# Memory tokens loaded transposed, with the norm's row factor applied behind the products, in a two-layer hybrid decoder on one core

## The chip, the cores and the metric

The kernel runs on one core of one Trainium2 chip. The metric is the device time of one execution in microseconds (us), as the median of three runs. The profile is of one execution. The engines are PE (matrix products; PEld is its weight load), DVE (vector), ACT (scalar, activations), POOL (GpSimd) and SP, which here issues most of the transfers.

## The reference, cut to what matters

All inputs are f32. `x` is 512 x 1024, `mem` is 256 x 1024.

```
mem_n = rmsnorm(mem, mem_norm_g)          # mem * rsqrt(mean(mem^2, row) + 1e-6) * g
for i in (0, 1):                          # layer 0: FoX attention; layer 1: retention
    h = rmsnorm(x, norm_g[i])
    q, k, v, (f_logit), q_mem, z = split(h @ w_in[i])
    main = fox_attention(...) or retention(...)          # 12 heads of 128
    kv = mem_n @ w_mem_kv[i]; km, vm = split(kv)         # 4 heads of 128 each
    memo = softmax(q_mem @ km.T / sqrt(128)) @ vm        # per head, 256 memory tokens
    x = x + (concat(main, memo) * silu(z)) @ w_out[i]
return rmsnorm(x, final_norm_g)
```

The change touches `mem_n`, `km` and `vm` alone. The row factor `rsqrt(mean + eps)` is one number for each memory token, and the gain `g` one for each of the 1024 channels.

## The kernel before

Each f32 product is made of three products of rounded parts: an operand is split into a high part H (a cast to the type float32r) and a low part L (the operand minus H), and `split3` lists (H, H), (H, L), (L, H). `split_to` does such a split with an ACT cast and a DVE subtraction.

Weights come as pieces of 128 x 1024 (512 KB) in the order of their use. `load_piece` has SP issue the load of the next piece into one of three raw buffers. `prep_piece` casts a raw piece to wH on ACT (L127), subtracts on DVE to wL (L128; four buffers of each) and then calls `load_piece`, whose transfer waits for the raw buffer. `retire` is called when PE is through with a piece, and prepares a further one.

The program is a list of cycles. A cycle is a list of filler chunks (dense products for PE) and of jobs that are put between the chunks at given positions; a job at position p is emitted behind the chunk in which p lies. PE's order is the order of emission, by hand (`MANUAL`). SP's is by hand during the first two cycles, and that of DVE, ACT and POOL in the opening block of `emit` (L795 to L801). All else on these three engines is placed by the scheduler, by priority and readiness.

The opening: `start_mem` issues the loads of the norm gain (as two rows of one partition), of the two halves of `mem` (128 tokens each, tokens on partitions), of the identity (`csb`) and of three pieces, and has POOL broadcast the gain to all partitions (L683). 13 products on zeros warm PE up (L794). `mem_norm(b)` calls `normed`: ACT squares the half and sums each row (L167), POOL makes the row factor with a TENSOR_SCALAR (L168) and a power (L169), and DVE multiplies by factor and gain (L170). `mem_T(b)` transposes the half on PE in eight blocks (L177) and splits it from PSUM into the tiles `mT` (L148, L149), which have channels on partitions.

The first cycle has eight chunks for layer 1: four of the values (`f_vm`, L387, 12 products of 512 columns each, in an order in which token half 0 comes first) and four of the keys (`f_km`, L59 by way of `mm_group`, 24 products of 256 columns each). The second half's transposes (`mem1`) are a job at position 1.5, and the loads of the first norm's gain and of `x` are jobs from position 2.5 on (`xload`). Layer 1's keys and values are written to DRAM for later. The second cycle has the same products for layer 0 and, between them, the norms and transposes of `x`. Then layer 0 begins.

Of the kernel before, what the change touches and what calls it, by code (L numbers as in the profile page):

```python
# [8 lines left out]
F32 = mybir.dt.float32  # L9
# [23 lines left out]


@with_exitstack
def tile_hybrid(ctx, tc, x_in, mem_in, norm_g, mem_g, fin_g, b_f, wv0, wp, index, consts, cosT, sinT, dec, out):
    nc = tc.nc
    P = 128
    KD = D // P
# [34 lines left out]
    def tile_(tag, shape, dt=F32):  # L74
        return work.tile(shape, dt, name=tag, bufs=BUFS[tag])

    csb = cst.tile([P, P], F32, name="csb")
    ident = csb[:, 0:P]
    nhalf = cst.tile([P, 1], F32, name="nhalf")
    G.memset(nhalf, -0.5)  # L80
# [15 lines left out]
    def load_g(ap):  # L96
        return load(ap.partition_broadcast(P))

# [1 line left out]
    order = []  # L100
    raws, pieces = {}, {}
    nload, nprep = [0], [0]
# [16 lines left out]
    def prep_piece():  # L119
        i = nprep[0]  # L120
        if i < len(order):
            key = order[i]
            n = 1072 if is_v0(key) else 1024
            raw = raws.pop(key)
            H = wpool.tile([P, 1072], F32R, name="wH", bufs=BUFS["w"])
            L = wpool.tile([P, 1072], F32R, name="wL", bufs=BUFS["w"])
            A.copy(out=H[:, :n], in_=raw[:, :n])  # L127
            V.tensor_tensor(out=L[:, :n], in0=raw[:, :n], in1=H[:, :n].bitcast(F32), op=ALU.subtract)  # L128
            pieces[key] = (H, L)
            nprep[0] += 1  # L130
            load_piece()
# [10 lines left out]
        retire(*retired)  # L142
        retired.clear()

# [13 lines left out]

    def acc_tile():
        return ps_at("acc", [P, 512], F32, name="acc")  # L160

    def normed(src, g, dst):
        ss = small.tile([P, 1], F32, name="ss")
# [22 lines left out]
                                    hL[:, hf * 4:hf * 4 + 4, t * P:(t + 1) * P], slice(0, 4))])  # L186
        yield

# [1 line left out]
    def f_T(key, done):  # L190
        box = {}

# [159 lines left out]
    def f_km(l, h):  # L352
        key = (l, "km", h)

        def fn():
            H, L = pieces[key]
            mT = st["mT"]
            ps = acc_tile()
            terms = []
            for w, c in ((H, 0), (H, 1), (L, 0)):  # L360
                for k in range(KD):
                    terms.append((w[:, k * P:(k + 1) * P], mT[k][c]))
            mm_group(ps[:, :NMEM], terms)
            kt = tile_("km", [P, 2, NMEM], F32R)
            split_to(kt[:, 0, :], kt[:, 1, :], ps[:, :NMEM])
            st[l, "km", h] = kt
            if l == 1:
                nc.sync.dma_start(out=km_d[h], in_=kt.bitcast(F32))
            retire(key)
        return [([key], fn)]  # L370

    def f_vm(l, plan):
        box = {}
        seen = {}

        def part(steps, final):
            mT = st["mT"]
            for i, b in steps:
                H, L = pieces[l, "vm", i]
                if b not in box:  # L380
                    box[b] = acc_tile()
                n = 0
                for k2 in range(2):
                    k = 2 * i + k2
                    for a, w in split3(mT[k][0][:, b * P:(b + 1) * P], mT[k][1][:, b * P:(b + 1) * P],
                                       H[:, k2 * 512:(k2 + 1) * 512], L[:, k2 * 512:(k2 + 1) * 512]):
                        PE.matmul(box[b], lhsT=a, rhs=w, start=(i == 0 and n == 0), stop=(i == 3 and n == 5))  # L387
                        n += 1
                seen[i] = seen.get(i, 0) + 1
                if seen[i] == 2:  # L390
                    retire((l, "vm", i))
            if final:
                vm = [tile_("vv", [P, 2, 512], F32R) for _ in range(2)]
                for b in range(2):
                    split_to(vm[0][:, b, :], vm[1][:, b, :], box[b])
                st[l, "vm"] = vm
                if l == 1:
                    for c in range(2):
                        nc.sync.dma_start(out=vm_d[c], in_=vm[c].bitcast(F32))
        res, used = [], set()  # L400
        for steps in plan:
            keys = [(l, "vm", i) for i, _ in steps if i not in used]
            keys = list(dict.fromkeys(keys))
            used.update(i for i, _ in steps)
            res.append((keys, lambda steps=steps, f=steps is plan[-1]: part(steps, f)))
        return res
# [13 lines left out]
            G.dma_start(out=vm[c], in_=vm_d[c])  # L420
        st[1, "vm"] = vm

# [175 lines left out]
    def g_forget():  # L598
# [42 lines left out]
        ret2=(0, 1, 2, 3, 5, 6, 8, 12),  # L641
        forget=(0, 2, 3),
        norm=(0, 2),
        mem1=(0,),
        xload=(0, 1, 2, 3, 4),
    )
    def mem1_gen():
        mem_T(1)
        prep_piece()
        yield  # L650

    GEN = dict(mem=g_mem, fox=g_fox, ret=g_ret, ret2=g_ret, forget=g_forget, norm=norm_gen, mem1=mem1_gen, xload=lambda: xload_gen())

    cycles = []
    tail_jobs = []
# [6 lines left out]
    def cycle(fillers, jobs=(), start=None, mode=None, last=False):  # L662
        cycles.append((fillers, jobs, start, mode, last))
# [2 lines left out]
        return [(kind, (l, h), base + i * gap) for i, h in enumerate(heads)]  # L666

    def start_mem():
        g1 = tile_("dd", [1, D // 2]), tile_("dd", [1, D // 2])
        for i in range(2):  # L670
            nc.sync.dma_start(out=g1[i], in_=mem_g[i * 512:(i + 1) * 512].unsqueeze(0))
        src = []
        for b in range(2):
            src.append(load(mem_in[b * P:(b + 1) * P, :]))
            if b == 0:
                nc.sync.dma_start(out=csb, in_=consts[:, 0:P])
                load_piece()
        for _ in range(BUFS["raw"] - 1):
            load_piece()
        st["msrc"] = src  # L680
        st["mg"] = tile_("vv", [P, D])
        for i in range(2):
            G.partition_broadcast(st["mg"][:, i * 512:(i + 1) * 512], g1[i])  # L683
        mT = [[tile_("gg", [P, 2, NMEM], F32R) for _ in range(2)] for _ in range(4)]
        st["mTt"] = mT
        st["mT"] = [(m[0][:, k, :], m[1][:, k, :]) for m in mT for k in range(2)]

    def mem_norm(b):
        xn = tile_("vv", [P, D])
        normed(st["msrc"][b], st["mg"], xn)  # L690
        st["mxn", b] = xn

    def mem_T(b):
        mT = st["mTt"]
        cs = slice(b * P, (b + 1) * P)
        transposes(st["mxn", b], lambda hf: [(mT[hf * 2 + k][0][:, :, cs], mT[hf * 2 + k][1][:, :, cs],
                                              slice(2 * k, 2 * k + 2)) for k in range(2)])

    def xload_gen():
        st["g", 0] = load_g(norm_g[0])  # L700
        yield
        for t in range(NT):
            nc.sync.dma_start(out=xt[t], in_=x_in[t * P:(t + 1) * P, :])
            yield

    def build_layer(l):
        M = "fox" if l == 0 else "ret"
        fq = (lambda pr: f_q(0, "q", pr * 2, NEG_SCALE) + f_q(0, "k", pr * 2, None) +
# [9 lines left out]
        for pr in range(6):  # L718
# [67 lines left out]
    def emit():  # L786
# [6 lines left out]
        for i in range(WARM):  # L793
            PE.matmul(wps, lhsT=warm[:, :P], rhs=warm, start=(i == 0), stop=(i == WARM - 1))  # L794
        with tc.manual_schedule(engines={mybir.EngineType.DVE, mybir.EngineType.Pool, mybir.EngineType.Activation}):  # L795
            mem_norm(0)
            prep_piece()
            mem_T(0)
            prep_piece()
            mem_norm(1)  # L800
            prep_piece()  # L801
# [145 lines left out]
```

## Time and profile before

| what | us |
|---|---|
| median of three runs | 962.19 (961.83 to 962.3) |
| span of the profiled execution, first to last instruction | 959.9 |
| PE busy in it | 932.4 (97%) |
| DVE busy | 592.2 (62%) |
| ACT busy | 435.5 (45%) |
| POOL busy | 36.8 (4%) |

The profiled execution was timed by its span only; 2.3 us lie between that and the median of the runs. A row of the timeline gives the start, the busy time, the engine, the line, the operation with its output and inputs and a count, and in brackets the idle time before it with what ended it. A row of groups gives the busy time and the mean duration of one in ns. A row of windows gives for each engine the busy time and the number of instructions, then PE's granted clock, the share of the DMA engines and the rate in GB/s.

### The profile page before, as it was taken

Reading aid. Unit: us, or ns where it says so; the run is one execution under the profiler, and the core shown is the slowest. Engines: PE = TensorE matmul, PEld = TensorE weight load, DVE = VectorE, ACT = ScalarE, POOL = GpSimd, SP = SyncE. Lnnn points to the kernel's source line nnn. Section 1 sums busy time; section 2 is a strip of 40 time slices with the busy share of each in tenths; the row PEclk is TensorE's granted clock in tenths of the full one; section 3 lists DMA queues with packets and bytes.
Section 4 is the critical chain, followed back from the end, with each engine's and each line's share of the span. In section 5 each row is a group of like instructions: output and inputs, shape, how many; then the busy total and the mean of one; then the engine's idle time right before and its main releaser. Section 6 shows DMA issues by size and latency. Waiting matters only on the chain.

```text
span 959.9 us, 13070 instructions
## 1 busy us (share of the span) xinstructions
PE 932.4 (97%) x5017; PEld 799.4 (83%) x5017; DVE 592.2 (62%) x1035; ACT 435.5 (45%) x746; POOL 36.8 (4%) x94
## 2 busy tenths in 40 slices
PE   3999999999999999999999999999999999999995
PEld 2899888888889889898888898888889889888984
DVE  2676655555655536645547766567768476856776
ACT  2564444432433324433425344455447354744554
POOL 1020100000000000000000010000000000000001
PEclk7999999999999999999999999999999999999998
DMA  4684322222323223222232242323332343333202
GB/s 140 244 316 138 127 82 97 98 78 83 103 79 99 78 89 90 86 67 99 99 109 79 66 154 67 106 71 98 99 99 77 99 121 108 113 99 97 91 23 88
DMA packets 32058, 99.69 MB, mean 104 GB/s; under 512 B 4206, under 2 KB 4462, under 8 KB 31996
## 3 DMA queue, kind: packets, MB, share of 16 engines
q1 hardware_dynamic: 30556, 95.72, 30.7%
q0 software_dynamic: 864, 2.10, 0.8%
q10 hardware_dynamic: 576, 1.05, 0.3%
q8 instruction: 39, 0.64, 0.3%
q14 instruction: 23, 0.19, 0.1%
HBM read 91.48 MB, written 4.22 MB: 100 GB/s over the span
## 4 chain that ended last, share of the span: by engine, by line
PE 95%; issue 2%; ACT 1%; DVE 1%; POOL 1%; DMA 0%; POOLq 0%; DVEq 0%; ACTq 0%
PE acc L201 44%; PE acc L59 33%; PE s L59 6%; PE o L491 5%; PE acc L387 2%; PE pt L525 1%; PE o L59 1%; PE pt L177 1%; PE pt L460 1%; PE acc L334 1%; PE acc L328 1%; ACT dd L762 0%; DVE p L565 0%; ACT vv L773 0%; DVE x L291 0%
## 5 line engine op out<-in xcount | busy, mean ns | idle before, releaser
L128 DVE TENSOR_TENSOR wL<-raw,wH 128x1024 fp32r<-128x1024 f32 x148 | 181.0, 1224 | 137.3 <-ACT wH L127 79.2
L127 ACT CAST wH<-raw 128x1024 fp32r<-128x1024 f32 x148 | 154.8, 1049 | 111.4 <-PE acc L201 54.6
L201 PE MATMUL acc<-hL,wH 128*128 128x512 f32 x608 | 164.3, 396 | 0.0
L201 PE MATMUL acc<-hH,wH 128*128 128x512 f32 x608 | 154.8, 396 | 0.0
L201 PE MATMUL acc<-hH,wL 128*128 128x512 f32 x608 | 152.4, 393 | 0.0
L59 PE MATMUL acc<-wH,gg 128*128 128x512 f32 x448 | 147.6, 397 | 0.0
L201 PEld LDWEIGHTS acc<-hH,wL 128*128 128x128 f32 x608 | 114.3, 188 | 26.1
L201 PEld LDWEIGHTS acc<-hL,wH 128*128 128x128 f32 x608 | 111.3, 188 | 21.9
L201 PEld LDWEIGHTS acc<-hH,wH 128*128 128x128 f32 x608 | 111.0, 188 | 22.1
L59 PE MATMUL acc<-wH,hH 128*128 128x256 f32 (+1 forms) x384 | 108.7, 283 | 0.0
L59 PE MATMUL acc<-wL,hH 128*128 128x256 f32 (+1 forms) x384 | 107.9, 281 | 0.0
L59 PE MATMUL acc<-wH,hL 128*128 128x256 f32 (+1 forms) x384 | 107.7, 280 | 0.0
L59 PEld LDWEIGHTS acc<-wH,gg 128*128 128x128 f32 x448 | 84.2, 188 | 18.4
L59 PE MATMUL acc<-wL,gg 128*128 128x512 f32 x224 | 88.2, 394 | 0.0
L291 DVE TENSOR_TENSOR x<-acc,x 128x512 f32<-128x512 f32 x80 | 55.0, 689 | 43.5 <-PE acc L59 41.3
L59 PEld LDWEIGHTS acc<-wL,hH 128*128 128x128 f32 x384 | 72.3, 188 | 0.5
L59 PEld LDWEIGHTS acc<-wH,hH 128*128 128x128 f32 x384 | 72.3, 188 | 0.5
L59 PEld LDWEIGHTS acc<-wH,hL 128*128 128x128 f32 x384 | 72.3, 188 | 0.0
L515 ACT ACTIVATE p<-dd,nm 128x128 f32<-128x128 f32 (+3 forms) x48 | 27.0, 563 | 66.6 <-DVE nm L511 66.5
L148 ACT CAST pTH<-pt 128x128 fp32r<-128x128 f32 (+2 forms) x64 | 29.7, 465 | 57.5 <-PE pt L525 44.6
L59 PE MATMUL s<-qk 128*128 128x256 f32 (+3 forms) x240 | 54.4, 327 | 0.6 <-DVE p L565 0.6
L148 ACT CAST gg<-sz 128x512 fp32r<-128x512 f32 x32 | 19.9, 621 | 75.7 <-PE acc L59 32.3
(148 smaller groups left out, 1190.0 us busy)
## 6 DMA issues: line engine op xcount, KB each, us to landing
raw<-in_wp_dram SPq DMA_DIRECT2D x146, 512.0 KB, 3.5
cbc<-c_d SPq DMA_DIRECT2D x12, 256.0 KB, 3.2
cbc<-in_dec_dram SPq DMA_DIRECT2D x12, 256.0 KB, 3.8
dd<-dd SPq DMA_DIRECT2D x48, 64.0 KB, 2.0
x<-in_x_dram SPq DMA_DIRECT2D x4, 512.0 KB, 8.4
raw<-in_wv_dram SPq DMA_DIRECT2D x2, 536.0 KB, 3.9
vv<-in_mem_dram SPq DMA_DIRECT2D x2, 512.0 KB, 4.6
vv<-in_norm_g_dram SPq DMA_DIRECT2D x2, 512.0 KB
```

The lines of the kernel that those rows point to most:

```text
L59: PE.matmul(ps, lhsT=l, rhs=r, start=(i == 0), stop=(i == n - 1))
L127: A.copy(out=H[:, :n], in_=raw[:, :n])
L128: V.tensor_tensor(out=L[:, :n], in0=raw[:, :n], in1=H[:, :n].bitcast(F32), op=ALU.subtract)
L148: A.copy(out=dH, in_=src)
L177: PE.transpose(pt[:, k, :], xn[:, c:c + P], ident)
L201: PE.matmul(box["ps"], lhsT=a[:, k * P:(k + 1) * P], rhs=b[:, k, :], start=(n == 0), stop=(n == 23))
L291: V.tensor_tensor(out=dst, in0=ps, in1=dst, op=ALU.add)
L328: PE.matmul(ps, lhsT=a, rhs=b, start=(i == 0), stop=False)
L334: PE.matmul(ps, lhsT=a, rhs=b, start=False, stop=(i == 2))
L387: PE.matmul(box[b], lhsT=a, rhs=w, start=(i == 0 and n == 0), stop=(i == 3 and n == 5))
L491: PE.matmul(o[:, j * P:], lhsT=a, rhs=b, start=(j == 0 and i == 0), stop=(j == NT - 1 and i == 2))
L515: A.activation(p[:, :n], dd[:, :n], AF.Exp, bias=nm, scale=-1.0, accum_out=sm)
```

## The change

`mem` is given to the kernel a second time, transposed on the host into two tiles of 128 x 4 x 256 (channels on partitions), and the gain as 128 x 8 columns. The transposed tiles are split as they land, with the gain as a factor for each partition, straight into `mT`. Products with them lack the row factor. That is computed from the row layout of `mem`, which is still loaded, behind the pieces; `rstd_of` makes one factor for each token half, and the values are split from PSUM with it as a scale for each partition. For the keys, whose tokens lie on the free axis, `spread` lays both factors out as a row on all partitions with two f32 products, and DVE multiplies by it (into `kn`) before the split. This runs as a job (`memr`) at position 1.5, where `mem1` stood. The values' chunks go piece by piece, both token halves in each. The `xload` jobs begin at position 0.5. Comments were taken out as well.

```
 def start_mem():
-    g1 = tile_("dd", [1, D // 2]), tile_("dd", [1, D // 2])
-    for i in range(2):
-        nc.sync.dma_start(out=g1[i], in_=mem_g[i * 512:(i + 1) * 512].unsqueeze(0))
-    src = []
-    for b in range(2):
-        src.append(load(mem_in[b * P:(b + 1) * P, :]))
-        if b == 0:
-            nc.sync.dma_start(out=csb, in_=consts[:, 0:P])
-            load_piece()
+    nc.scalar.dma_start(out=gc, in_=g_cols)
+    src = [tile_("vv", [P, 4, NMEM]) for _ in range(2)]
+    rows = [tile_("vv", [P, D]) for _ in range(2)]
+    nc.sync.dma_start(out=src[0], in_=memT_in[0])
+    load_piece()
+    nc.sync.dma_start(out=src[1], in_=memT_in[1])
     for _ in range(BUFS["raw"] - 1):
         load_piece()
-    st["mg"] = tile_("vv", [P, D])
-    for i in range(2):
-        G.partition_broadcast(st["mg"][:, i * 512:(i + 1) * 512], g1[i])
+    nc.sync.dma_start(out=csb, in_=consts[:, 0:P])
+    for b in range(2):
+        nc.sync.dma_start(out=rows[b], in_=mem_in[b * P:(b + 1) * P, :])
...
-def mem_norm(b):
...
-def mem_T(b):
...
+def mem_split(k):
+    dH, dL = st["mT"][k]
+    split_to(dH, dL, st["msrc"][k // 4][:, k % 4, :], gc[:, k:k + 1])
+
+def memr_gen():
+    st["mr"] = [rstd_of(st["mrows"][b], st["mrows"][b], f"mr{b}") for b in range(2)]
+    spread(st["mr"], rbm)
+    yield
...
+def rstd_of(src, junk, name):
...
+    A.activation(junk, src, AF.Square, accum_out=ss)
+    G.tensor_scalar(out=r, in0=ss, scalar1=1.0 / D, scalar2=EPS, op0=ALU.mult, op1=ALU.add)
+    G.tensor_tensor(out=r2, in0=r, in1=nhalf, op=ALU.pow)
+    return r2
+
+def spread(rs, dst):
+    pb = ps_at("t", [P, 4, P], F32, name="pt")
+    for i, r in enumerate(rs):
+        PE.matmul(pb[:, i, :], lhsT=r.to_broadcast([P, P]), rhs=ident, start=True, stop=True)
+    n = len(rs)
+    A.copy(out=dst[:, :n * P], in_=pb[:, :n, :].rearrange("p n c -> p (n c)"))
...
 # f_km
-            split_to(kt[:, 0, :], kt[:, 1, :], ps[:, :NMEM])
+            kn = tile_("dd", [P, 512])
+            V.tensor_tensor(out=kn[:, :NMEM], in0=ps[:, :NMEM], in1=rbm, op=ALU.mult)
+            split_to(kt[:, 0, :], kt[:, 1, :], kn[:, :NMEM])
 # f_vm
-                    split_to(vm[0][:, b, :], vm[1][:, b, :], box[b])
+                    split_to(vm[0][:, b, :], vm[1][:, b, :], box[b], st["mr"][b])
...
-    cycle(f_vm(1, [[(0, 0), (1, 0)], [(2, 0)], [(0, 1), (1, 1)], [(2, 1), (3, 0), (3, 1)]]) +
-          sum([f_km(1, h) for h in range(4)], []), [("mem1", (), 1.5), ("xload", (), 2.5)], mode=8)
+    cycle(f_vm(1, [[(i, 0), (i, 1)] for i in range(4)]) +
+          sum([f_km(1, h) for h in range(4)], []), [("memr", (), 1.5), ("xload", (), 0.5)], mode=8)
...
 # emit, with DVE, POOL and ACT in hand order
-            mem_norm(0)
-            prep_piece()
-            mem_T(0)
-            prep_piece()
-            mem_norm(1)
-            prep_piece()
+            for i in range(4):
+                mem_split(2 * i)
+                mem_split(2 * i + 1)
+                prep_piece()
```

## Rows read from the trace of the kernel before

**Rows 1.** The page: PE's busy tenths in 40 slices, and the chain by engine.
```profile
PE   3999999999999999999999999999999999999995
...
PE 95%; issue 2%; ACT 1%; DVE 1%; POOL 1%; DMA 0%; POOLq 0%; DVEq 0%; ACTq 0%
```

**Rows 2.** Windows: the stretch behind the opening.
```profile
29.93:950.00 920.07, 918.63 (x4969) 789.51 (x4970) 578.32 (x1017) 422.84 (x724) 31.60 (x77) 1.00 0.32 102
```

**Rows 3.** Windows: two stretches of the opening.
```profile
6.40:18.60 12.20, 0.00 (x0) 0.00 (x0) 1.33 (x2) 1.04 (x1) 2.26 (x4) 0.58 0.35 138
18.60:29.93 11.33, 8.51 (x35) 6.32 (x35) 7.50 (x10) 5.64 (x10) 0.74 (x2) 0.85 0.40 123
```

**Rows 4.** Timeline of the opening, all engines.
```profile
4.82 1.06 ACT L167 ACTIVATE vv<-vv 128x1024 f32<-128x1024 f32 x1 [2.82 <-DMA vv<-in_mem_dram]
...
7.33 1.04 ACT L127 CAST wH<-raw 128x1024 fp32r<-128x1024 f32 x1 [1.36 <-DMA raw<-in_wp_dram]
7.83 1.48 POOL L683 PARTITION_BROADCAST vv<-dd  x2 [6.98 <-issue]
16.37 0.18 POOL L168 TENSOR_SCALAR rstd<-ss 128x1 f32<-128x1 f32 x1 [7.06 <-issue]
...
18.47 1.22 DVE L128 TENSOR_TENSOR wL<-raw,wH 128x1024 fp32r<-128x1024 f32 x1
...
18.61 1.97 PE L177 MATMUL pt<-csb,vv 128*128 128x128 f32 x8 [12.31 <-DVE vv L170]
```

**Rows 5.** Timeline of SP: its issues.
```profile
0.73 0.65 SPq L671 DMA_DIRECT2D dd<-in_mem_norm_g_dram  x2
1.42 0.35 SPq L93 DMA_DIRECT2D vv<-in_mem_dram  x1
...
4.83 0.56 SPq L810 DMA_DIRECT2D bfb<-in_fox_b_f_dram  x1
19.71 15.99 SPq L115 DMA_DIRECT2D raw<-in_wp_dram  x6
```

**Rows 6.** Timeline: layer 1's first key products, and a row factor of x.
```profile
36.99 2.07 PE L59 MATMUL acc<-gg,wH 128*128 128x256 f32 x16
...
50.39 0.19 ACT L167 ACTIVATION_READ_ACCUMULATOR vv<-x 128x1 f32 x1
...
50.94 0.55 POOL L169 TENSOR_TENSOR rstd<-rstd,nhalf 128x1 f32<-128x1 f32 x1
```

**Rows 7.** Groups by shape, 0 to 72 us.
```profile
L128 DVE TENSOR_TENSOR wL<-raw,wH 128x1024 fp32r<-128x1024 f32 x16 | 19.4, 1222 | 6.0 <-ACT wH L127 6.0
L127 ACT CAST wH<-raw 128x1024 fp32r<-128x1024 f32 x16 | 16.6, 1051 | 7.7 <-DMA raw<-in_wp_dram 5.9 <-PE acc L387 1.2 <-PE acc L59 0.7
...
L149 DVE TENSOR_TENSOR km<-acc,km 128x256 fp32r<-128x256 f32 x8 | 3.3, 417 | 0.0
...
L148 ACT CAST km<-acc 128x256 fp32r<-128x256 f32 x8 | 2.9, 366 | 0.7 <-PE acc L59 0.7
```

**Rows 8.** Groups by shape, whole span, ACT.
```profile
L773 ACT ACTIVATE vv<-vv,rstd 128x512 f32<-128x512 f32 x4 | 2.9, 719 | 2.7 <-POOL rstd L768 2.7
```

**Rows 9.** DMA view, 0 to 12 us, in 40 slices: rate, and what moved.
```profile
GB/s 0 0 0 0 0 7 7 0 96 177 314 410 410 336 333 369 341 328 273 150 205 150 177 355 437 410 396 382 396 423 410 437 410 430 397 289 173 3 0 0
DMA packets 1156, 2.83 MB, mean 236 GB/s; under 512 B 258, under 2 KB 514, under 8 KB 1156
```

**Rows 10.** Windows: the first 72 us and stretches of it.
```profile
0.00:72.00 72.00, 55.44 (x335) 48.75 (x336) 40.06 (x49) 35.64 (x55) 9.73 (x22) 0.91 0.67 233
30.00:72.00 42.00, 42.00 (x288) 38.80 (x289) 30.67 (x38) 26.46 (x41) 6.41 (x10) 1.00 0.84 299
30.00:36.80 6.80, 6.80 (x30) 5.44 (x31) 5.33 (x8) 4.79 (x7) 0.00 (x0) 1.00 0.54 179
48.40:61.40 13.00, 13.00 (x114) 13.00 (x113) 8.79 (x13) 10.21 (x19) 4.81 (x9) 1.00 0.97 373
61.40:72.00 10.60, 10.60 (x53) 8.80 (x52) 9.40 (x11) 5.97 (x8) 1.60 (x2) 1.00 0.79 242
```

More of the change, by code (lines that the diff above doesn't have):

```diff
@@ L35, in tile_hybrid @@
 @with_exitstack
-def tile_hybrid(ctx, tc, x_in, mem_in, norm_g, mem_g, fin_g, b_f, wv0, wp, index, consts, cosT, sinT, dec, out):
+def tile_hybrid(ctx, tc, x_in, mem_in, memT_in, g_cols, norm_g, fin_g, b_f, wv0, wp, index, consts, cosT, sinT, dec, out):
     nc = tc.nc
@@ L77, in tile_hybrid @@
     csb = cst.tile([P, P], F32, name="csb")
+    gc = cst.tile([P, KD], F32, name="gc")
+    rbm = cst.tile([P, NMEM], F32, name="rbm")
     ident = csb[:, 0:P]
@@ L160, in acc_tile @@
         return ps_at("acc", [P, 512], F32, name="acc")
+    def rstd_of(src, junk, name):
+        ss = small.tile([P, 1], F32, name="ss")
+        r = small.tile([P, 1], F32, name="rstd")
+        r2 = small.tile([P, 1], F32, name=name, bufs=1)
+        A.activation(junk, src, AF.Square, accum_out=ss)
[8 more added lines that the diff above has]
+        A.copy(out=dst[:, :n * P], in_=pb[:, :n, :].rearrange("p n c -> p (n c)"))
     def normed(src, g, dst):
@@ L643, in tile_hybrid @@
         norm=(0, 2),
-        mem1=(0,),
+        memr=(0,),
         xload=(0, 1, 2, 3, 4),
     )
-    def mem1_gen():
-        mem_T(1)
-        prep_piece()
-        yield
-    GEN = dict(mem=g_mem, fox=g_fox, ret=g_ret, ret2=g_ret, forget=g_forget, norm=norm_gen, mem1=mem1_gen, xload=lambda: xload_gen())
+    GEN = dict(mem=g_mem, fox=g_fox, ret=g_ret, ret2=g_ret, forget=g_forget, norm=norm_gen, memr=lambda: memr_gen(), xload=lambda: xload_gen())
     cycles = []
@@ L668, in start_mem @@
     def start_mem():
-        g1 = tile_("dd", [1, D // 2]), tile_("dd", [1, D // 2])
-        for i in range(2):
-            nc.sync.dma_start(out=g1[i], in_=mem_g[i * 512:(i + 1) * 512].unsqueeze(0))
-        src = []
-        for b in range(2):
-            src.append(load(mem_in[b * P:(b + 1) * P, :]))
-            if b == 0:
-                nc.sync.dma_start(out=csb, in_=consts[:, 0:P])
-                load_piece()
+        nc.scalar.dma_start(out=gc, in_=g_cols)
[4 more added lines that the diff above has]
+        nc.sync.dma_start(out=src[1], in_=memT_in[1])
         for _ in range(BUFS["raw"] - 1):
             load_piece()
-        st["msrc"] = src
-        st["mg"] = tile_("vv", [P, D])
-        for i in range(2):
-            G.partition_broadcast(st["mg"][:, i * 512:(i + 1) * 512], g1[i])
+        nc.sync.dma_start(out=csb, in_=consts[:, 0:P])
+        for b in range(2):
+            nc.sync.dma_start(out=rows[b], in_=mem_in[b * P:(b + 1) * P, :])
+        st["msrc"], st["mrows"] = src, rows
         mT = [[tile_("gg", [P, 2, NMEM], F32R) for _ in range(2)] for _ in range(4)]
@@ L686, in start_mem @@
         st["mT"] = [(m[0][:, k, :], m[1][:, k, :]) for m in mT for k in range(2)]
-    def mem_norm(b):
-        xn = tile_("vv", [P, D])
-        normed(st["msrc"][b], st["mg"], xn)
-        st["mxn", b] = xn
-    def mem_T(b):
[L694 to L697, printed above, removed]
+    def mem_split(k):
[5 more added lines that the diff above has]
+        yield
     def xload_gen():
@@ L795, in emit @@
         with tc.manual_schedule(engines={mybir.EngineType.DVE, mybir.EngineType.Pool, mybir.EngineType.Activation}):
-            mem_norm(0)
-            prep_piece()
-            mem_T(0)
-            prep_piece()
-            mem_norm(1)
-            prep_piece()
+            for i in range(4):
+                mem_split(2 * i)
+                mem_split(2 * i + 1)
+                prep_piece()
         carry = []
@@ L929 @@
                             axis=1).astype(np.float32)
-    ins = [("x", np.asarray(x)[0]), ("mem", np.asarray(mem)[0]), ("norm_g", np.asarray(norm_g)),
-           ("mem_norm_g", np.asarray(mem_norm_g)), ("final_norm_g", np.asarray(final_norm_g)),
+    xs, ms = np.asarray(x)[0], np.asarray(mem)[0]
+    memT = ms.T.reshape(2, 4, 128, 256).transpose(0, 2, 1, 3)
+    gcols = np.asarray(mem_norm_g).reshape(8, 128).T
+    ins = [("x", xs), ("mem", ms), ("memT", memT), ("gcols", gcols), ("norm_g", np.asarray(norm_g)),
+           ("final_norm_g", np.asarray(final_norm_g)),
            ("fox_b_f", np.asarray(fox_b_f)[0]), ("wv0", np.stack(wv0)), ("wp", wp),
@@ L941 @@
     o = nc.dram_tensor("out_0_dram", (512, 1024), F32, kind="ExternalOutput").ap()
-    xa, ma, ng, mg, fg, bf, v0, wpa, ca, ct, st, de = aps
+    xa, ma, mta, gca, ng, fg, bf, v0, wpa, ca, ct, st, de = aps
     with tile.TileContext(nc, schedule_with_timeline_sim=TLS) as tc:
-        tile_hybrid(tc, xa, ma, ng, mg, fg, bf, v0, wpa, index, ca, ct, st, de, o)
+        tile_hybrid(tc, xa, ma, mta, gca, ng, fg, bf, v0, wpa, index, ca, ct, st, de, o)
     r = run_bass_kernel_spmd(nc, [arrays], core_ids=[0])
```

## The prediction

> **What bounds the kernel now.** I read the page's slices and chain first [rows 1]. PE is the engine of the chain (95%), and its row shows 9 in every slice but the first and the last, so the first thing to ask is whether anything but PE's own work costs time after the opening. The stretch from 29.93 us to 950 us answers it [rows 2]: PE is busy 918.63 of 920.07 us at a granted clock of 1.00 (2.4 GHz). Whatever PE starts earlier at 30 us therefore arrives whole at the end, and an edit off PE there is worth nothing. The opening is different [rows 3]: from 6.40 to 18.60 us PE does nothing at all, and from 18.60 to 29.93 us it is busy 8.51 of 11.33 us, at a mean clock of 0.85.
>
> The timeline of the first 30 us says why [rows 4]. The first half of the memory is in at 4.82 us (ACT squares it then), and the first weight piece at 7.33 us (ACT casts it). But POOL sits 6.98 us with no operand named ("issue") before its two partition broadcasts of the norm gain, and 7.06 us in the same way before its next instruction, the row factor's TENSOR_SCALAR, at 16.37 us. DVE's normalisation waits for that factor, and behind it, in DVE's hand-written order, stands the subtraction that finishes the first piece: it runs at 18.47 us, though the piece's cast was done at 8.37 us. PE's first transposes come at 18.61 us. So the opening is bound by POOL, not by transfers: SP, whose three raw buffers are full, issues nothing between 4.83 and 19.71 us [rows 5].
>
> My meeting point is the first key product of layer 1, whose run begins at 36.99 us [rows 6]. From there on both kernels run the same PE work.
>
> **The change, part by part.** *Removed on POOL:* both broadcasts, with both 7 us gaps. *Removed on PE:* 16 transposes; the first eight took 1.97 us [rows 4]. *Removed on ACT and DVE:* the normalisation and the splits of transposed tiles. In their place are eight splits of 128x256 with a gain per partition. The nearest rows are an ACT cast of that size without a factor, 366 ns [rows 7], and one of 128x512 with a factor, 719 ns [rows 8]; between these bounds I take 0.50 us. On DVE I take 0.42 us, as for a subtraction of 128x256 [rows 7].
>
> *Transfers of the opening.* Before, bytes flow from about 2.4 us, 1.0 us after the memory's first issue at 1.42 us [rows 5], until about 11.1 us (the view's 40 slices are 0.3 us each): 2.83 MB in 8.7 us, 0.325 MB/us [rows 9]. The first 0.524 MB by this rate end at 4.0 us and are seen at 4.82 us, so 0.8 us goes to completion. Piece 0 checks the rule: its 512 KB end 1.12 MB into the queue, which gives 6.6 us, and 7.33 us was measured, an error of 0.7 us. After the change the first big issue is SP's first instruction (0.73 us), so bytes flow from 1.7 us, and in SP's order there land: transposed half 0 at 4.1 us, piece 0 at 5.7 (6.4 with the error), half 1 at 7.3, piece 1 at 9.0, piece 2 at 10.6, the identity at 10.8, the two row tiles at 12.4 and 14.0, and piece 3 at 16.0 us. The row tiles are 1.05 MB that the change adds. The gain columns are 4 KB, 32 bytes for a partition, on ACT's own queue. No row shows such a load. The memory's half, 128 times larger, took 3.4 us from its issue to its use, so from an issue near 0.7 us the columns are there by 4.1 us, under the cover of half 0; without that cover each microsecond costs one.
>
> *First products.* Splits 0 and 1 are done at 5.9 us. Piece 0 is cast from 6.4 to 7.45 us and subtracted to 8.7 us (1.05 and 1.22 us, [rows 7]); PE starts in earnest at 8.7 us. A value chunk is 12 products of 512 columns at 0.227 us (30 in 6.80 us, [rows 10]), 2.72 us. Chunk 0 ends at 11.4 us if the clock holds. It may not: the mean of 0.58 from 6.40 to 18.60 us is 1.95 us at 1.00 and the rest at 0.50, so 2.4 GHz lasted to 8.35 us, and the mean of 0.85 after the restart is 3.4 us at 0.50 [rows 3]. Then chunk 0 ends at 13.1 us. Piece 1 is ready at 11.3 us, so chunk 1 ends between 14.1 and 15.8 us.
>
> *The new wait.* PE's order is written by hand, and behind chunk 1 stand two small products ("spread") that need both row factors. All later PE work queues behind them. ACT is through with the splits and pieces 1 and 2 at 13.1 us, then squares the row tiles in 1.06 + 0.19 us each [rows 4, 6], the second from 14.35 to 15.6 us (it landed at 14.0). From such an accumulator's end to the end of POOL's power takes 0.91 us (50.58 to 51.49 us, [rows 6]): 16.5 us. The two products are plain f32. Eight transposes of that size took 1.97 us in the slow stretch [rows 4], 0.25 us each, so I take 0.5 us for the two (0.25 at full rate, were they no dearer than transposes): 17.0 us. The Trainium skill ("FP8 and Floating Point Precision", TensorE Precision Notes) says that true FP32 takes four passes through the array; by it they would be some 1.0 us at full rate (an estimate, four times the transposes) and the end 0.5 us later. No run here shows it yet.
>
> *Sum.* Chunks 2 and 3 take 24 x 0.227 = 5.45 us: first key product at 22.5 us. Piece 3 (16.0 + 1.05 + 1.22 = 18.3 us) is there when chunk 3 begins at 19.7 us, and piece 4, whose raw buffer is free at 11.3 us, by 20 us. 36.99 - 22.5 = 14.5 us gained. If PE's wait before the spread, 0.7 to 2.4 us, costs the clock again, 1.7 us goes (3.4 us at half rate). I put that at a third and take 14.0 us.
>
> *Costed at nothing.* Eight multiplications by the factors' row, 0.42 us on DVE each, stand between a key product and its split. DVE is busy 30.67 of the 42 us from 30 to 72 us [rows 10], 34 with them (81%), and they free the PSUM tile sooner than the old subtraction did. Without that cover they cost 3.4 us. The factor in the value split replaces a cast of the same tile, 0.13 us dearer twice per layer at most. The x loads move two chunks earlier in SP's order, behind the load of piece 7; the weights behind them come later by 0.524/0.325 = 1.6 us for each, and four pieces lie split ahead of PE as cover.
>
> The profiled span is 959.9 us, 2.3 us under the median of 962.19 us; both lose the same. **Forecast: 945.9 us of span, 948.2 us timed.**
>
> **The rivals.**
> *A: the factor is late.* The squares are free to be placed by the scheduler, and piece 3's cast, in hand order, may stand ahead of them on ACT. It lands at 16.0 us; the squares then end at 19.55 us, POOL at 20.5, the spread at 21.0, and the clock has fallen (+1.7): key products from 28.1 us, gain 8.9, **953.3 us**. For: an engine works strictly in its order, as DVE's subtraction shows, which stood 10 us behind a late factor [rows 4]. Against: the row tiles are issued first and land first. With one square on either side, some 951 us.
>
> *B: POOL pays at first use.* If TENSOR_SCALAR waits 7.06 us again when its operand is there, the spread ends at 24.0 us, and with the slow clock key products begin at 31.2 us: gain 5.8, **956.4 us**. For: both gaps of rows 4. Against: 6.98 us fits a start at 0.85 us, before any operand, and a later factor shows no such gap [rows 6]. The Trainium skill ("GPSIMD Engine Reference", 2.1 Instruction dispatch) says that the first call to a freshly loaded kernel pays a load of about 6 us. The trace's gaps, 6.98 and 7.06 us, agree; by that rule the price would come once more only if POOL's arithmetic isn't resident when the program starts.
>
> *C: transfers bind the opening.* By 72 us the kernel had moved 233 x 72 = 16.8 MB [rows 10]; with the row tiles it must move 17.8 MB by 58 us, from 1.7 us on: 317 GB/s. From 48.4 to 61.4 us 373 GB/s flowed [rows 10], so there is room of some 8 us. Below 17.8/70.3 = 253 GB/s the gain is gone, and at the 242 GB/s of the last window of rows 10 the time is **965.5 us**, slower than now. Against: that low rate stood with SP waiting for free buffers.
>
> *D: the gain is no gain.* If PE work after 30 us waits for x's norm by as much as was won, the time is as before. Only an x load 14 us late would do that.
>
> **How the numbers follow.** Forecast with its neighbours (clock held or lost, 945.5 to 950.5) 0.62; one or both squares behind piece 3 0.22; B 0.06; C 0.06, half of it slower; D 0.02; something unseen that makes it slower 0.02. The lower end is PE without any wait: 8.7 + 10.9 + 0.5 gives 20.1 us, 16.9 gained, 945.3, and I put 945.5. The upper end takes in A with 1.7 us of error: 955. That leaves B, C and D out. Faster by over 0.2% (1.9 us, about what a measurement of this kernel can tell from no change) 0.93, within it 0.02, slower 0.05.
>
> **What would show it.** Right: no broadcast and no 7 us gap on POOL; the first earnest product near 8.7 us; the spread near 16.5 us, waiting for POOL; layer 1's key products from 22 to 23 us; PE full from there on. Wrong: squares behind piece 3 on ACT (A), a gap on POOL after the square (B), ACT casts that wait for raw transfers while PE starves between 25 and 60 us (C), or a DVE that runs late there.

## The result, and the profile after

The changed kernel takes 947.8 us (median of four runs, 946.96 to 947.99), against 962.01 us for the kernel before (961.64 to 962.3): a ratio of 0.9851, interval [0.9838, 0.9865]. The forecast was 948.2 us, and 945.9 us of span; the profiled span is 946.0 us.

The page of the changed kernel: PE's tenths, and the chain by engine [rows 1].

```profile
PE   8999999999999999999999999999999999999996
...
PE 92%; ACT 1%; DVE 1%; POOL 0%; issue 0%; POOLq 0%; DVEq 0%; ACTq 0%
```

PE's first slice went from 3 to 8 tenths and the last one from 5 to 6; nothing between them shows a difference. The windows show more: span, then busy time and count of PE, PEld, DVE, ACT and POOL, the granted clock, the DMA share and GB/s.

```profile
6.40:12.00 5.60, 3.67 (x9) 2.67 (x9) 5.15 (x9) 5.60 (x11) 0.00 (x0) 0.71 1.03 413
12.00:18.60 6.60, 6.60 (x31) 5.40 (x30) 3.49 (x5) 5.04 (x8) 1.82 (x4) 0.99 0.79 265
18.60:29.93 11.33, 11.33 (x83) 10.66 (x82) 8.04 (x11) 6.51 (x11) 0.15 (x1) 1.00 0.82 291
29.93:45.00 15.07, 15.07 (x129) 15.04 (x128) 11.69 (x18) 8.56 (x16) 3.94 (x9) 1.00 0.89 352
45.00:58.00 13.00, 12.16 (x63) 9.79 (x62) 10.83 (x14) 8.85 (x12) 1.16 (x2) 1.00 0.81 256
58.00:936.00 878.00, 876.57 (x4683) 750.48 (x4682) 547.97 (x980) 396.36 (x683) 25.01 (x67) 1.00 0.30 93
```

Where PE did nothing before [rows 3], it is busy 3.67 of 5.60 us and then without a gap. But one row has a hole that the prediction did not have: from 45 to 58 us PE is busy 12.16 of 13.00 us. That is the stage in which x's norms are made between layer 0's key and value products.

The timeline of the opening, all engines [rows 4]:

```profile
4.47 1.28 ACT L153 ACT_TABLE_LOAD   x1 [4.47 <-DMA vv<-in_memT_dram]
5.76 0.91 ACT L153 ACTIVATE gg<-vv,gc 128x256 fp32r<-128x256 f32 x2
...
6.58 1.03 ACT L129 CAST wH<-raw 128x1024 fp32r<-128x1024 f32 x1
...
8.92 0.79 PE L407 MATMUL acc<-wL,gg 128*128 128x512 f32 x1 [0.76 <-DVE wL L130]
...
11.82 1.04 ACT L168 ACTIVATE vv<-vv 128x1024 f32<-128x1024 f32 x1
...
12.86 1.04 ACT L168 ACTIVATE vv<-vv 128x1024 f32<-128x1024 f32 x1
13.04 0.52 POOL L169 TENSOR_SCALAR rstd<-ss 128x1 f32<-128x1 f32 x1 [12.19 <-ACT vv L168]
...
13.90 1.03 ACT L129 CAST wH<-raw 128x1024 fp32r<-128x1024 f32 x1
...
14.55 0.56 POOL L170 TENSOR_TENSOR mr<-rstd,nhalf 128x1 f32<-128x1 f32 x1
...
15.85 0.60 PE L176 MATMUL pt<-csb,mr 128*128 128x128 f32 x4
16.21 0.48 PE L407 MATMUL acc<-wH,gg 128*128 128x512 f32 x1
...
21.89 0.51 PE L59 MATMUL acc<-gg,wH 128*128 128x256 f32 x3
```

POOL starts its row factor as soon as ACT's sum is there (13.04 us), with no 7 us gap behind it. Both squares stand ahead of piece 3's cast (13.90 us). The factors are done at 15.11 us, before PE is through with chunk 1, so the spread (four records for its two products) waits for nothing. The first key product is at 21.89 us instead of 36.99 [rows 6]: 15.10 us earlier. The transfers ran faster than I had worked out [rows 9]:

```profile
GB/s 0 0 0 0 0 55 218 109 234 261 248 385 414 411 437 396 437 410 369 423 437 437 423 423 396 410 410 437 425 328 463 410 396 410 423 396 396 410 410 437
DMA packets 1341, 3.92 MB, mean 327 GB/s; under 512 B 272, under 2 KB 400, under 8 KB 1341
```

Not all of the 15.10 us arrives at the end. The first product with x, of 268 columns, before the change and after it:

```profile
74.25 0.37 PE L59 MATMUL acc<-wH,hH 128*128 128x268 f32 x1
...
60.70 0.37 PE L59 MATMUL acc<-wH,hH 128*128 128x268 f32 x1
```

It stood 37.26 us behind the first key product, and now stands 38.81 us behind it. So 1.55 us is given back between these two points (I call the stretch between them the x stage). From there to the end 885.65 us have become 885.30; where these 0.35 us come from wasn't traced. The balance of the span: 15.10 - 1.55 + 0.35 = 13.90 us, which is 959.9 - 946.0.

The timeline of the place where most of the 1.55 us goes:

```profile
42.76 0.20 ACT L185 ACTIVATION_READ_ACCUMULATOR vv<-x 128x1 f32 x1
...
44.42 0.42 DVE L384 TENSOR_TENSOR dd<-acc,rbm 128x256 f32<-128x256 f32 x1
...
44.92 0.41 ACT L150 CAST km<-dd 128x256 fp32r<-128x256 f32 x1 [1.95 <-issue]
...
45.31 1.05 ACT L129 CAST wH<-raw 128x1024 fp32r<-128x1024 f32 x1
...
46.42 0.50 PE L407 MATMUL acc<-wH,gg 128*128 128x512 f32 x1
46.49 1.22 DVE L130 TENSOR_TENSOR wL<-raw,wH 128x1024 fp32r<-128x1024 f32 x1
...
47.76 0.50 PE L407 MATMUL acc<-wL,gg 128*128 128x512 f32 x1 [0.84 <-DVE wL L130]
```

PE is at the first value chunk of layer 0 at 46.42 us, and the low part of its piece comes from DVE only at 47.71 us. DVE could not subtract earlier because ACT cast the piece at 45.31 us. ACT stood idle for 1.95 us before that, with a key's cast at the head of its order, and this key's cast needs DVE's new multiplication (44.42 us). PE's second product stands 1.34 us behind the first; before the change it stood 0.32 us behind it (61.41 and 61.73 us).

### The profile page after: what moved, and what is told of

It is laid out like the page before. It is cut to its first block, busy times and chain, and to the rows that moved or that the text cites. A ratio compares the mean times of both kernels' runs of the same rounds, so it can differ in the third digit from the quotient of the medians.

```text
span 946.0 us, 13062 instructions
## 1 busy us (share of the span) xinstructions
PE 931.2 (98%) x5005; PEld 798.1 (84%) x5005; DVE 592.5 (63%) x1041; ACT 436.5 (46%) x747; POOL 34.4 (4%) x92
## 4 chain that ended last, share of the span: by engine, by line
PE 92%; ACT 1%; DVE 1%; POOL 0%; issue 0%; POOLq 0%; DVEq 0%; ACTq 0%
PE acc L219 45%; PE acc L59 31%; PE s L59 6%; PE o L511 5%; PE pt L545 1%; PE acc L407 1%; PE o L59 1%; PE pt L480 1%; PE acc L352 1%; PE acc L346 1%; PE pt L195 1%; ACT dd L771 0%; DVE p L585 0%; ACT vv L782 0%; DVE x L309 0%
```

## The experiments

All are timed against the kernel before on the same chip (medians 961.72 to 962.17 us). "Key" is the start of the first key product and "x" that of the first product of 268 columns, from the profiled execution. Each of these is one execution; those of the changed kernel lie 1.0 us apart, and not all kernels ran on the same chip. So a difference of less than 1 us between two medians below shows nothing by itself, and such differences are read from the traces.

| kernel | median us (range) | ratio, interval | key | x | x - key |
|---|---|---|---|---|---|
| before | 962.01 (961.64 to 962.3) | | 36.99 | 74.25 | 37.26 |
| after | 947.8 (946.96 to 947.99) | 0.9851 [0.9838, 0.9865] | 21.89 | 60.70 | 38.81 |
| e1 | 953.13 (952.04 to 953.73) | 0.9905 [0.9891, 0.9918] | 28.46 | 65.71 | 37.25 |
| e2 | 955.97 (951.82 to 957.12) | 0.9928 [0.9909, 0.9947] | 26.01 | 64.80 | 38.79 |
| e3 | 946.27 (945.82 to 946.77) | 0.9835 [0.9822, 0.9848] | 21.18 | 58.91 | 37.73 |
| e4 | 947.42 (947.04 to 947.75) | 0.9846 [0.9833, 0.9860] | 21.98 | 60.12 | 38.14 |
| e5 | 947.47 (947.12 to 948.26) | 0.9853 [0.9838, 0.9867] | 21.13 | 60.32 | 39.19 |
| e6 | 947.04 (946.73 to 947.62) | 0.9848 [0.9833, 0.9862] | 20.25 | 59.93 | 39.68 |
| e7 | 947.43 (947.38 to 947.99) | 0.9852 [0.9838, 0.9867] | 21.78 | 60.88 | 39.10 |
| e8 | 949.54 (949.44 to 949.61) | 0.9873 [0.9856, 0.9889] | 25.24 | 62.48 | 37.24 |
| e9 | 947.7 (946.87 to 947.8) | 0.9846 [0.9832, 0.9859] | 21.98 | 60.66 | 38.68 |
| e10 | 946.38 (946.33 to 946.9) | 0.9834 [0.9821, 0.9848] | 20.28 | 59.64 | 39.36 |
| e11 | 946.52 (946.45 to 947.31) | 0.9845 [0.9832, 0.9858] | 20.28 | 59.38 | 39.10 |
| e12 | 946.86 (946.3 to 949.09) | 0.9849 [0.9836, 0.9863] | 20.26 | 59.16 | 38.90 |

**e1: the kernel before, its gain loaded by one transfer instead of POOL's broadcasts.** It tells apart the two parts of the change: the broadcasts that go, and the transposed layout.

```diff
-    st["mg"] = tile_("vv", [P, D])
-    for i in range(2):
-        G.partition_broadcast(st["mg"][:, i * 512:(i + 1) * 512], g1[i])
+    st["mg"] = load_g(mem_g)      # 512 KB, behind half 0 of mem
```

> The kernel before with one thing changed: the norm gain is loaded to all partitions by one transfer of 512 KB, and POOL's two broadcasts are gone. Tokens stay on partitions, with the normalisation and the 16 transposes. Theory (the opening was bound by POOL's two 7 us gaps): the row factor is ready near 7 us in place of 17.2, the first transposes begin near 8.5 us in place of 18.61, and nearly all of that stays: about 10 us faster than before, 952 us. Rival (it is the transposed layout, with the chain of normalising, transposing and splitting gone, that gives the time): 2 us at most, 960 us.

Measured: 953.13 us, near the theory's 952. Its timeline:

```profile
5.72 0.19 POOL L168 TENSOR_SCALAR rstd<-ss 128x1 f32<-128x1 f32 x1 [4.87 <-ACT vv L167]
...
6.82 1.28 DVE L170 SCALAR_TENSOR_TENSOR vv<-vv,rstd 128x1024 f32<-128x1024 f32 x1 [5.43 <-DMA vv<-in_mem_norm_g_dram]
...
8.16 1.09 PE L177 MATMUL pt<-csb,vv 128*128 128x128 f32 x8 [1.07 <-DVE vv L170]
```

The row factor starts at 5.72 us (16.37 before [rows 4]), as soon as ACT's sum is there, and POOL had been idle for only 4.87 us. So 8.9 of the 14.2 us come from replacing the broadcasts by a transfer, in the old layout; the rest of the change gives the other 5.3 us.

**e2: the changed kernel with both broadcasts put back**, into a tile of x that is loaded later, so that they feed nothing.

```diff
+    g1 = tile_("dd", [1, D // 2]), tile_("dd", [1, D // 2])
+    for i in range(2):
+        nc.sync.dma_start(out=g1[i], in_=...)     # 2 KB each, first in SP's order
...
+    for i in range(2):
+        G.partition_broadcast(xt[3][:, i * 512:(i + 1) * 512], g1[i])
```

> The changed kernel with the two broadcasts of the gain put back on POOL, into a tile that nobody reads before x overwrites it. Theory (each gap starts where POOL's queue reaches it, with no regard to operands): broadcasts at 7.8 to 9.3 us, the first row factor's TENSOR_SCALAR at 16.4 us in place of 13.04, both factors at about 17.9 us, the spread at 18 us in place of 15.6; the changed kernel loses 2.4 us, and up to 4.1 if PE's clock falls in the wait: 950 to 952 us. Rival (the gap before TENSOR_SCALAR starts only when its operand is there, at 13 us): factors at 21.5 us, 954 us or more.

Measured: 955.97 us, but its four executions lie between 951.82 and 957.12 us, and the profile is of the fastest. In that one:

```profile
8.61 2.25 POOL L700 PARTITION_BROADCAST x<-dd  x2 [7.75 <-issue]
13.66 0.19 ACT L168 ACTIVATION_READ_ACCUMULATOR vv<-vv 128x1 f32 x1
...
18.26 0.18 POOL L169 TENSOR_SCALAR rstd<-ss 128x1 f32<-128x1 f32 x1 [7.40 <-issue]
...
20.09 0.49 PE L176 MATMUL pt<-csb,mr 128*128 128x128 f32 x2 [0.43 <-POOL mr L170]
...
49.45 1.06 ACT L129 CAST wH<-raw 128x1024 fp32r<-128x1024 f32 x1
50.62 1.22 DVE L130 TENSOR_TENSOR wL<-raw,wH 128x1024 fp32r<-128x1024 f32 x1
51.89 0.50 PE L407 MATMUL acc<-wL,gg 128*128 128x512 f32 x1 [0.84 <-DVE wL L130]
```

Both gaps are back, on broadcasts that nobody waits for. The second begins where the broadcasts end (10.86 us), and the operand that the row factor needs was there at 13.85 us, in the middle of it. So in this execution the gap runs from POOL's change between the two kinds of work, not from an operand. The key products come 4.1 us later. That is the upper end of the theory (950 to 952 us), but not by the theory's way, in which 1.7 of the 4.1 us came from PE's clock: chunks 2 and 3 take 5.68 us here as in the changed kernel, and it is the factors that are later than worked out, since the gaps are 7.75 and 7.40 us and the broadcasts 2.25 us long (6.98, 7.06 and 1.48 before [rows 4]). The other three executions take 3.8 to 5.3 us more. There is no trace of one, and their 955.6 to 957.1 us are what the rival forecast (954 or more). So the rival is refuted for the traced execution only.

**e3: the changed kernel without the key multiplication in layer 0** (layer 0's keys then lack the row factor). Layer 1's is kept.

```diff
+            if l == 0:
+                split_to(kt[:, 0, :], kt[:, 1, :], ps[:, :NMEM])
+            else:
...
```

> The changed kernel without the multiplication of layer 0's keys by the factors' row (they are split from PSUM as before; left out of the computation). Theory (the four multiplications in the stage of x's norms chain ACT's key casts to DVE, and PE's wait of 0.84 us and its slow restart at 46.4 us come from that): PE's wait at the first value chunk of layer 0 goes, 1.4 us faster than the changed kernel, 946.4 us. Rival (that wait comes from x's loads and norms being earlier in the order): no change, 947.8 us.

Measured: 946.27 us, near the theory's 946.4, but only in part for the theory's reason. Of the 1.79 us by which the first product of x is earlier, 0.71 us was won before the first key product. PE kept the upper clock there (compare the clock, 0.71 in this window after the change):

```profile
6.40:12.00 5.60, 4.24 (x17) 2.89 (x16) 5.14 (x9) 5.60 (x11) 0.00 (x0) 1.00 1.03 412
```

and then waited 0.43 us for the factors. The other 1.08 us is the x stage's: 37.73 us, so 0.47 us of the loss stays without the multiplications.

**e4: the loads of x at their old place** (`xload` at 2.5 instead of 0.5).

> The changed kernel with the loads of the first norm's gain and of x back at position 2.5. Theory (multiplications on DVE make the wait at 46.4 us): within 0.5 us of the changed kernel, 947.3 to 948.3 us. Rival (the earlier x loads push weight pieces back, so DVE gets piece 12 late): the wait goes and the kernel is 1.4 us faster, 946.4 us.

Measured: 947.42 us, at the lower edge of the theory and within the range of the changed kernel's runs. The x stage loses 0.88 us instead of 1.55, and PE's wait at the value chunk is gone. In its place PE waits 0.61 us for a key multiplication on DVE at 25.61 us. So the wait at the value chunk went, as the rival had it, and the time that the rival put on it did not come.

**e5 and e6: an earlier start.** e5 has 20 warm-up products instead of 13. e6 has these and the spread behind chunk 3 instead of chunk 1.

```diff
-WARM = 13
+WARM = 20
...
-        memr=(0,),
+        memr=(0, 2),        # e6, with a yield ahead of spread()
```

> The changed kernel with 20 warm-up products in place of 13, so that PE works until some 8 us and the clock should still be at 2.4 GHz when the first value chunk starts. Theory (the chunk at half rate costs up to 1.7 us, but the spread behind chunk 1 then waits for the row factors, which are ready at 15.1 us): chunk 1 ends near 14 us, the first key product comes at 21.2 us in place of 21.9, 0.7 us faster, 947.1 us. Rival (the chunks are bound by the splits on DVE, not by PE's clock): no change, 947.8 us.

> The same with 20 warm-up products and the spread moved behind chunk 3 in PE's order (the row factors themselves stay where they were). Theory (with the clock held only the spread's wait is left): PE never waits after 8.9 us, the first key product comes near 20.5 us, 1.4 us faster than the changed kernel, 946.4 us. Rival (the late spread delays the keys' factors and so the first key's leaving of PSUM): the gain of the earlier start is lost again by 45 us, 947.1 us or more.

Measured: 947.47 and 947.04 us. The key products started 0.76 and 1.64 us earlier, as the two theories had it, and 0.38 and 0.87 us more was lost in the x stage, as the rival of e6 had it for the time. In these two traces about half of the earlier start is given back. In e6 PE's waits there are again for DVE's part of a weight piece (0.54 and 0.87 us); that the late spread makes them, as the rival says, isn't shown, since e5, without it, waits 0.25 and 0.84 us at the same places.

**e7: the keys' low part on POOL instead of DVE.**

```diff
-            split_to(kt[:, 0, :], kt[:, 1, :], kn[:, :NMEM])
+            A.copy(out=kt[:, 0, :], in_=kn[:, :NMEM])
+            G.tensor_tensor(out=kt[:, 1, :], in0=kn[:, :NMEM], in1=kt[:, 0, :].bitcast(F32), op=ALU.subtract)
```

> The changed kernel with the low part of the keys (the product times the factor, minus its high part, both in SBUF) subtracted on POOL in place of DVE. Theory (DVE's eight added multiplications are what makes piece 12 late in the stage of x's norms): DVE has as much to do there as before the change, PE's wait of 0.84 us at 46.4 us goes or shrinks, 1 us faster, 946.8 us. Rival (it is the chain from DVE's multiplication to ACT's key cast that holds ACT, whoever subtracts; or POOL is slow with two inputs and holds x's row factors): no change or slower, 947.8 us or more.

Measured: 947.43 us; the x stage loses 1.84 us, no less than in the changed kernel. Taking eight subtractions off DVE did not help. But this does not settle whether DVE's load is the cause: POOL takes 1.19 us for one in the mean (DVE 0.41), and while POOL works on one (45.11 to 46.81 us), DVE's subtraction for the value chunk's piece takes 1.76 us (46.14 to 47.90) instead of 1.22. PE's wait there is 1.27 us. Without the 0.54 us more, the loss would be near 1.3 us (an estimate from these rows).

**e8: rival A made on purpose.** The squares are put into the hand order behind piece 3's cast.

> The changed kernel with the row factors' squares put behind piece 3's cast in ACT's hand order: rival A of the prediction made by hand. By the prediction's price (piece 3 lands at 16.0 us): spread at 21.0 us, 5 to 6 us slower than the changed kernel, 953 us. By the trace after the change (transfers at about 0.41 MB/us, piece 3 cast at 13.9 us behind the squares): the cast goes from 12.9 us, squares end at 16.3, the spread begins at 17.2 in place of 15.6 us: 1.6 us slower, 949.4 us.

Measured: 949.54 us, which is the 949.4 worked out from the trace of the changed kernel, and 3.8 us below the 953.3 of the prediction. Its timeline, and two of its windows:

```profile
16.73 0.49 PE L176 MATMUL pt<-csb,mr 128*128 128x128 f32 x2 [2.22 <-POOL mr L170]
...
17.78 0.49 PE L176 MATMUL pt<-csb,mr 128*128 128x128 f32 x2 [0.56 <-POOL mr L170]
...
25.24 0.99 PE L59 MATMUL acc<-gg,wH 128*128 128x256 f32 x7
...
44.84 2.00 ACT L129 CAST wH<-raw 128x1024 fp32r<-128x1024 f32 x2
...
47.37 1.22 DVE L130 TENSOR_TENSOR wL<-raw,wH 128x1024 fp32r<-128x1024 f32 x1
...
49.66 0.48 PE L407 MATMUL acc<-wH,gg 128*128 128x512 f32 x1
...
49.97 0.40 PE L407 MATMUL acc<-wL,gg 128*128 128x512 f32 x1
```

```profile
18.60:25.24 6.64, 6.64 (x23) 5.22 (x22) 3.15 (x4) 2.76 (x4) 0.00 (x0) 0.74 0.77 266
...
45.00:62.00 17.00, 17.00 (x102) 14.85 (x101) 14.40 (x20) 10.42 (x15) 0.86 (x2) 1.00 0.76 227
```

PE waits 2.78 us for the factors, and the clock falls behind the wait (0.74), as the rival had it: chunks 2 and 3 take 7.22 us (18.02 to 25.24) instead of 5.68. So the key products come 3.35 us later, not 1.6, and that the time fits the 949.4 is luck, for the x stage gives 1.57 us of it back. It loses nothing here (37.24 us), with all the multiplications in it. Here ACT casts the value chunk's piece at 44.84 us, the next one right behind it, and DVE has its low part at 48.59 us, 23.35 us after the first key product. In the changed kernel that was 25.82 us. It is not the later start that helps: e2 starts at 26.01 us, with ACT's order as in the changed kernel, has the low part 25.83 us after the first key product, and loses 1.53 us. DVE's load doesn't tell the two apart either. DVE's busy time (the third of the busy times) up to the first value chunk, in the changed kernel and in e8:

```profile
21.90:47.80 25.90, 25.06 (x211) 24.70 (x209) 20.49 (x30) 16.57 (x27) 5.24 (x10) 1.00 0.88 333
...
25.24:51.10 25.86, 25.86 (x215) 25.63 (x214) 20.99 (x31) 17.19 (x28) 5.46 (x10) 1.00 0.90 321
```

So in these traces the loss goes with the place of one piece's cast in ACT's order, which the scheduler chose anew in e8: ahead of a key's cast that waits for DVE, or behind it. No run moves that cast alone, so that the place is the cause isn't shown.

**e9 and e10: layer 0's values ahead of its keys**, e9 in the changed kernel and e10 in e6.

```diff
-    cycle(sum([f_km(0, h) for h in range(4)], []) + f_vm(0, [[(i, 0), (i, 1)] for i in range(4)]),
+    cycle(f_vm(0, [[(i, 0), (i, 1)] for i in range(4)]) + sum([f_km(0, h) for h in range(4)], []),
```

> The changed kernel with the products of the second stage in another order: layer 0's value chunks ahead of its key chunks. The theory is that the 1.55 us given back in the stage of x's norms come from VectorE, whose key multiplications and key subtractions fall into the same stretch as x's norms and the splits of the weight pieces; with the values (whose factor rides in the two operations that they need anyhow) first, and the keys after them when the norms are nearly done, TensorE should wait under 0.5 us between the first key product and the first 128x268 product, and the time should be about 946.5. The rival is that ScalarE and the weight pieces set the pace of that stretch whatever stands in it: then the loss stays at about 1.5 us and the time at 947.5 to 948.

> The same order of products, with 20 opening warm-up products instead of 13 and the spread of the row factors put behind the fourth value chunk, which alone brought the first key product from 21.89 to 20.25 us but gave 2.42 us back. By the theory (VectorE's load in that stretch) the earlier start is now kept: 944.5 to 945.5. By the rival (the pieces set the pace) the end of the stretch stays where it was and the time is 946.5 to 947.5.

Measured: 947.7 and 946.38 us, e9 at the rival's time and e10 just under the rival's 946.5 to 947.5. The theory of DVE's load falls: the loss is 1.42 and 2.10 us, hardly less than in the same kernels with the keys first (1.55 and 2.42). The waits have only moved. PE's waits in e10:

```profile
PE acc L59 <- DVE wL L130: 0.6, 1, 0.6
PE acc L407 <- DVE wL L130: 0.5, 1, 0.5
```

**e11 and e12: x loaded later in e10 and in e6** (`xload` at 2.5).

> e10 with x's four row tiles loaded later (start 2.5 instead of 0.5 in the schedule of the first stage). e9 and e10 refuted the theory that VectorE's load by itself makes the loss: with the values first the loss was still 1.4 and 2.1 us. The theory now is that the stretch is set by weight pieces that are late, because 2 MB of x tiles pass the same 16 DMA engines (share 1.01 from 30 to 40 us) ahead of them, and because ScalarE stands before operations whose product is not there with a landed piece's cast behind them. With x later TensorE's waits in the stretch should fall from 1.75 us to about 1 us or less, and the time from 946.4 to 945.6. The rival, that the order of the operations on ScalarE and VectorE alone decides, whatever has landed, leaves the waits and the time where they are, 946.4.

> The same later loads of x, with the key chunks first as in the changed kernel (e6 with start 2.5). By the theory of late pieces e6's waits of 1.4 us go down and the time from 947.0 to about 946.2. By the rival it stays at 947.0.

Measured: 946.52 us, which is e10's time and the rival's, and 946.86 us, between the two (its executions go from 946.3 to 949.09, and the trace is of the fastest). In both the late waits for pieces are gone, and e12 has PE full from 30 to 60 us. In both new waits stand near the start of the keys, for DVE; the two of e12:

```profile
23.98 2.12 PE L59 MATMUL acc<-gg,wH 128*128 128x256 f32 x16 [0.61 <-DVE dd L384]
...
27.59 2.17 PE L59 MATMUL acc<-gg,wH 128*128 128x256 f32 x16 [0.55 <-DVE vv L154]
```

So the theory of late pieces is half right: what it removed was there, and what it gained went into another wait.

## Why the prediction was right

The time was right to 0.4 us, and the span to 0.1 us. The mechanism was right: POOL's gaps bound the opening, and the change removed them. That the sum fits to 0.1 us is luck, since its errors cancel: the key products came 0.6 us earlier than forecast, the 0.5 us set aside for the clock were not needed, 0.35 us was won at the end, and 1.55 us was lost in a stage that the prediction had put at nothing.

- *What bounds the opening.* Right: POOL's gaps. e1 removes them in the old kernel and gets 8.9 us; e2 puts them back and loses 4.0 us in its fastest execution.
- *"Whatever PE starts earlier arrives whole."* This step failed, by 1.55 us. Rows 2 showed PE full at the old start, with ACT and DVE far enough ahead. The step took that for a property of the stage. In the new schedule ACT's and DVE's work there lets PE wait (0.84 us at 47.76 us), and the traces of e5 and e6 show that a further gain of 0.76 and 1.64 us comes through by half.
- *Transfers.* The rate was mis-sized: 325 GB/s (0.325 MB/us) forecast from a stretch with slices of 150 to 205 GB/s in it [rows 9], 413 GB/s measured from 6.40 to 12.00 us. The half tile was in at 4.47 us (4.1 forecast), piece 0 was cast at 6.58 (6.4), the squares began at 11.82 and 12.86 (13.1 and 14.35), and piece 3 was cast at 13.90 us (landing 16.0 forecast).
- *First products.* 8.92 us for 8.7, and chunk 1 ends at 15.85 us, at the edge of the forecast 14.1 to 15.8. The clock fell for chunk 0, as the slower case had it. ACT's table load was not in the sum: 1.28 us from 4.47 us on, so that splits 0 and 1 were done at 7.19 us instead of 5.9. It cost little, for piece 0's cast behind them still began at 6.58 us.
- *The new wait.* It did not come in this kernel: factors at 15.11 us instead of 16.5. The spread costs PE 0.36 us (15.85 to 16.21) for the 0.5 taken, and e3 and e5, where PE was faster, do wait 0.43 and 0.42 us. Of the Trainium skill's rule ("FP8 and Floating Point Precision", TensorE Precision Notes: four passes for true FP32): the 1.0 us that I made of it was not seen. At the upper clock eight transposes take 0.79 us here (38.95 to 39.74 us), 0.10 us each, and a spread product took 0.18 us. So the error was to count a transpose as one pass and a product as four of it: the product costs 1.8 transposes. How many passes it makes no row shows; each has two records.
- *Sum.* Forecast: key products at 22.5 us, 0.5 us off for the clock, 14.0 us. Measured: 21.89 us, nothing off for the clock behind the spread, 1.55 us off in the x stage, 0.35 us back behind it, 13.9 us.
- *Costed at nothing.* The multiplications take 420 ns each, as worked out. Their cover did not hold in full: without the four of layer 0 the x stage is 1.08 us shorter (e3), of the 1.7 us that four cost if nothing covers them. It can hold: e8 has all eight and loses nothing. So their price hangs on the order around them. The prediction named "a DVE that runs late there" as a sign against it, with no price.

The rivals: A did not occur, and was priced too high (e8: 1.7 us instead of 5.1). Its way was right, with the clock's 1.7 us (1.54 measured); the spread was done at 18.02 us instead of 21.0, since the row tiles and piece 3 came earlier than forecast, and the x stage lost nothing there. B did not occur: POOL's arithmetic has no gap behind its operand at 13.04 us. A gap ahead of the operand could hide in POOL's 12.19 us of idle time there, but not in the 4.87 us of e1, where no broadcast stands before the row factor either. By the Trainium skill's rule ("GPSIMD Engine Reference", 2.1 Instruction dispatch: a load of about 6 us at the first call of newly loaded code) the broadcast's gap would be such a load, and its 6.98 us before and 7.75 us in e2 are of that size; no row shows what POOL does in it. The traces add that ordinary arithmetic behind it pays again, 7.06 and 7.40 us. C did not occur: with 265 to 352 GB/s flowing PE is full from 12.00 to 45.00 us, and its wait behind that (47.76 us) is for DVE. D did not occur as it was put: PE waits for a weight piece's low part, not for x's norm. It shares with D that a part of the gain, a tenth, is lost behind 30 us.

What stays open is the x stage. The runs show that the loss is not made by the multiplications alone (e8 has them all and loses nothing), nor by DVE's load alone (e8, e9), nor by the loads of x alone (e11). They point at the order on ACT and DVE (e2 against e8), but no run changes that order and nothing else. Why the scheduler lays out one order or the other wasn't traced. The fastest kernel that computes everything, e10, has 946.38 us: 1.4 us under the changed kernel, with ranges that don't overlap. But the two ran on different chips, the intervals of their ratios overlap, and it is less than the 0.2% that I hold to be told from no change.

## What to carry to other kernels

A broadcast on POOL between ordinary POOL arithmetic cost two gaps of 7 us here; at the start of a kernel, where nothing covers them, look for another way for the data (a transfer, or a factor for each partition). A row factor can be applied behind the product, so that the transfer alone stands ahead of PE. And "PE is full from here on" is a statement on one schedule: when its start moves earlier, look at how far ahead of it the casts and subtractions of its next operands are done, and price the stage in which that lead is smallest.

## What was not expected of the hardware

- POOL's gap started when POOL arrived at the instruction, whatever its operand did: 7.40 us in the traced execution of e2, over an operand that came 3.0 us into it.
- The clock of the same opening differs between executions of kernels that have the same 13 warm-up products and the same first chunks: 0.71 from 6.40 to 12.00 us in the changed kernel, 0.68 in e2 and 0.73 in e4, but 1.00 in e3 and e8. In e3 it is worth 0.7 us at the first key product. Why it differs isn't shown.
- ACT's table load of 1.28 us ran at 0.72 us in the kernel before, ahead of any data. After the change it ran at 4.47 us, only when the transposed tile had landed, and the first split waits behind it (5.76 us).
